# Operands of the MLP products of an encoder layer: from pairs of 32-bit planes to pairs of fp16 planes with scales found on the chip

## The chip, the cores and the metric

The kernel runs on one core of one Trainium2 chip. The metric is the device time of one execution in microseconds (us). A core has five engines that run side by side, each through its own instructions in order: TensorE (PE; its weight loads are shown apart as PEld), VectorE (DVE), ScalarE (ACT), GpSimd (POOL) and SyncE (SP). SP, ACT and POOL also issue DMAs, each on its own queue.

## What is computed

One layer of an encoder is applied to two sequences of 1024 and 512 tokens, 1024 features wide, in 32-bit floats. Two attention mixers come first; the change touches only the MLP behind them, and the norm that feeds it:

```python
def _rmsnorm(x, g):
    y = x * lax.rsqrt(jnp.mean(x * x, axis=-1, keepdims=True) + EPS)
    return y * g

h = h + _token_mixer(_rmsnorm(h, norm_mix_g), ...)          # attention, gates, projections
hn = _rmsnorm(h, norm_mlp_g)                                 # (1536, 1024)
h = h + jnp.square(jax.nn.relu(hn @ w_mlp_up)) @ w_mlp_down  # (1024, 4096), (4096, 1024)
out = _rmsnorm(h, norm_final_g)
```

## The kernel before, in words

Every 32-bit operand of a large product is held as two planes, `hi` and `lo`. `hi` is the value rounded to the 32-bit type that the code calls F32R (fp32r in the profile), `lo` is what is left. `mm3` (lines 273 to 276) makes a product of three matmuls: hi·hi, hi·lo, lo·hi. A plane pair is cut by two instructions: ACT copies the source into `hi`, and DVE subtracts `hi` from the source into `lo` (`cut`, lines 1564 to 1566).

The mixers of the two sequences run first, in a function `run` that is called once for each; at the end of the second, the norm for the MLP is formed token tile by token tile (gains in the tile `gb`), written to memory (`hnd`), read back as `hn` tiles, transposed by PE and cut into operands `B` (`pair_t`, lines 397 to 435).

`mlp` (from line 1541) computes the MLP with one level of a fast scheme that replaces 8 products of half-size blocks by 7. The 1536 tokens are two blocks `b` of 768 (384 columns in a half block). The up weights come in 16 chunks of 256 columns; one chunk of one block is a **stage**. `run_up` (line 1819) goes through the 16 stages of a block:

- `up_dma` (line 1587) loads the raw chunk `rawu` two chunks ahead on SP's queue, in two pieces of 512 KB.
- `up_steps` (line 1610) makes the seven operands A0 to A6 of the next chunk: four sums `S` on DVE and seven cuts. These steps are spread over the stage.
- `up` (line 1645) runs seven products of 4 x 3 matmuls with 384 columns: a (A0), b (A1), c (A2), d (A3), c again (A4), d again (A6), a again (A5). So a stage has 84 matmuls. Between them ACT and DVE empty PSUM: ACT copies `s` out of `ua` and `uc`, DVE adds, ACT takes relu and square (lines 1681 to 1685) and sends the result to memory (`ud`); DVE adds both halves (`cs`, line 1675), which SP stores.

Each engine takes its instructions in the order in which a scheduler put them when the kernel was built. In block 0, four stages (2, 4, 6 and 8) also hold a late norm of a token tile (`late_norm`, a sum of squares of 128x1024 on ACT, line 353).

Between the blocks stand three `pair_t` for block 1 and a first part of the down product (`dnf`, 144 matmuls of 512 columns). After block 1 the down product follows (`dn`, 1872 matmuls): stages of 6 x 12 matmuls with 512 columns, for which SP loads raw pieces `ar` (from `ud`) and `br` (down weights), DVE forms sums of them, and ACT and DVE cut them (`a_step`, line 1753, and `b_steps`, line 1773). DVE adds the results to the residual (`gain`), and a norm ends the kernel.

Of the kernel before, what the change touches and what calls it, by code (L numbers as in the profile page):

```python
# [11 lines left out]
F32 = mybir.dt.float32  # L12
# [62 lines left out]
def encoder(ctx: ExitStack, tc: tile.TileContext, xs, outs, w):  # L75
# [47 lines left out]
    gtab = cst.tile([P, 5, HD], F32, name="gtab")  # L123
    mhalf = cst.tile([P, 8], F32, name="mhalf")
# [3 lines left out]
    biases = dram.tile([8, 16, 8, 16, 48], F32, name="biases")  # L128

# [263 lines left out]
    def new_b(b, B):  # L393
        for i in range(7):
            B[i] = bbs[0].tile([P, 2, 4, HB], F32R, tag="bb", name=f"B{b}_{i}")

    def pair_t(nm, j, tiles, B, banks, tmp):
# [15 lines left out]
        def lo(i, src, eng=nc.vector):  # L413
            eng.tensor_tensor(B[i][:, 1, :, cols], v(src), B[i][:, 0, :, cols].bitcast(F32), op=ALU.subtract)
# [86 lines left out]
    def run(tr, nxt, first):  # L501
# [564 lines left out]
        with phase(f"phB{N}") as ph:  # L1066
# [228 lines left out]

            prep(0)
# [12 lines left out]
            for i in range(n + LS + LV):  # L1309
# [21 lines left out]
                fill.pull(f // 2)  # L1331
                if 0 <= i - LS < n:
                    t_unit(units[i - LS])
# [24 lines left out]
        with phase(f"phG{N}") as ph:  # L1358
# [72 lines left out]
            gb = gb[:, 0]  # L1431
            gn = None
# [6 lines left out]
            for half in range(2):  # L1439
                wo = wos[half]  # L1440
                hc = slice(half * 512, half * 512 + 512)
                for tt in range(NT):
# [65 lines left out]
                    if half == 1:  # L1508
# [5 lines left out]
                        if nxt is None:  # L1514
# [10 lines left out]
                            if 3 <= tt <= 5:  # L1525
                                j = tt - 3
                                if j == 2:
                                    a0 = first_a0.pop().tile([P, 2, 4, P], F32R, name="A0_0_0")
                                    nc.scalar.activation(a0[:, 0], a11, AF.Copy)
                                    nc.vector.tensor_tensor(a0[:, 1], a11, a0[:, 0].bitcast(F32), op=ALU.subtract)  # L1530
# [10 lines left out]
    def mlp():  # L1541
# [26 lines left out]

        def hn_load(b, j):
# [17 lines left out]
        def up_dma(st):  # L1587
            res = []
            for i in range(2):
                if st == (0, 0) and i == 1:  # L1590
# [10 lines left out]
                nc.sync.dma_start(  # L1601
                    r,
                    w["w_mlp_up"][0][i * 512 : (i + 1) * 512, st[1] * FB : (st[1] + 1) * FB].rearrange(
                        "(k p) c -> p k c", p=P
                    ),
                )
# [3 lines left out]
        def up_steps(st, ops):  # L1610
# [7 lines left out]
            def one(i):  # L1618
# [3 lines left out]
                t = k4.tile([P, 2, 4, P], F32R, tag="k4", name=f"A{nm}_{i}")  # L1622
# [11 lines left out]
                cut(t[:, 0], t[:, 1], src)  # L1634
# [10 lines left out]
        def up(st, A, B, side):  # L1645
# [27 lines left out]
            def total(half):  # L1673
                t = t2(f"cs{half}_{nm}")[:, 0:HB]
                nc.vector.tensor_tensor(t, kept[0, half], kept[1, half], op=ALU.add)
                nc.sync.dma_start(ud[b][2][fb // 4][fb % 4, :, half * HB : (half + 1) * HB], t)

            def put(f, half, src, in1=None):
# [6 lines left out]
                nc.scalar.activation(t, t, AF.Square)  # L1685
# [67 lines left out]
        def a_step(p, g, j):  # L1753
# [3 lines left out]
            hi, lo = (t2(f"a{n_}{p}_{g}_{j}", (P, 4, P), F32R) for n_ in "hl")  # L1757
            cut(hi, lo, r[0][:, :, (j % 2) * P : (j % 2 + 1) * P])
            a_hl[p, g, j] = (hi, lo)
# [13 lines left out]
        def b_steps(p, g):  # L1773
# [3 lines left out]
            def one(i):  # L1777
# [6 lines left out]
                t = k4.tile([P, 2, 512], F32R, tag="k4", name=f"wd{p}_{g}_{i}")  # L1784
                cut(t[:, 0], t[:, 1], src[:, i % 2, :])
# [33 lines left out]
        def run_up(b, A, B, last):  # L1819

            for fb in range(NFB):
                An = {}
                if fb + 2 < NFB:
                    up_dma((b, fb + 2))
                side = up_steps((b, fb + 1), An) if fb + 1 < NFB else []
                side = side + last(fb)
                if (b, fb) == (0, 0):
                    side = [[], []] + spread(side, 5)
                else:
                    side = spread(side, 7)  # L1830
                up((b, fb), A, B, side)
# [24 lines left out]
        def late_norm(r0):  # L1856
            xn = raw_k4(f"xnl{r0}")
            norm_to(xn, hl.pop(r0), gl[0][:, 0, :], f"l{r0}")
# [27 lines left out]
        for q in range(3):  # L1886
# [17 lines left out]
            for i in range(2):  # L1904
                j = 2 * q + i
                t = dp[:, i * 512 : i * 512 + 512]
                nc.scalar.activation(t, o[i], AF.Copy)
# [11 lines left out]

        hs = [bb.tile([P, 3, D], F32, tag="bb", name=f"hs{q}") for q in range(4)]  # L1920
# [46 lines left out]
        def final_last(o, e, t, before):  # L1967
# [15 lines left out]
            held(nc.vector.tensor_tensor(h[:, 0:512], o, h[:, 0:512], op=ALU.add))  # L1983
            square(ls, 1)
            before[0]()
            held(nc.vector.tensor_tensor(h[:, rs], e, h[:, rs], op=ALU.add))
# [29 lines left out]
        def gain(o, b, half, j):  # L2016
            t = b * NTB + j
            h = hs[t // 3][:, t % 3, half * 512 : half * 512 + 512]
            return nc.vector.tensor_tensor(h, o, h, op=ALU.add)
# [10 lines left out]
        for i, (p, g, j) in enumerate(order):  # L2030
# [16 lines left out]
            if i + 1 == len(order):  # L2047
# [10 lines left out]
                break  # L2058
            down_mm(acc[j], p, g, j, fresh, g == NG - 1)
# [7 lines left out]
            if g == NG - 1:  # L2067
                b, half = DEST[p][0]
                op = gain(acc[j], b, half, j)
# [4 lines left out]
                for b, half in DEST[p][1:]:  # L2074
                    todo.append(lambda o=acc[j], b=b, half=half, j=j: gain(o, b, half, j))
# [76 lines left out]
```

## Time and profile before

| | |
|---|---|
| median of 3 runs | 2090.28 us (2089.08 to 2093.42) |
| the profiled execution: its own time | 2090.06 us |
| its span (first to last instruction) | 2088.3 us |
| up product, block 0 / block 1 (about) | 1152 to 1386 us / 1423 to 1656 us |
| down product `dn` (about) | 1656 to 2080 us |

A profile is of one execution. A timeline row gives start, duration, engine, line, operation, output<-inputs, the shape and how many instructions were merged; in brackets stands how long the engine was idle before and what released it. A row of groups gives count, then busy time and mean duration, then idle time before. In a row for a tile or line the three numbers are the shortest, median and longest duration in ns. A row of windows gives for each stretch of time the busy time of PE, PEld, DVE, ACT and POOL, then the granted clock of TensorE (1.00 is full), the mean busy share of the 16 DMA engines and GB/s. Matmuls overlap: how often one starts says how fast PE goes, not how long one is shown.

### The profile page before, as it was taken

The page shows a single profiled execution, that of the slowest core. Times are in us where ns is not written, and L with a number is a line of the kernel's source. Part 1 is how long each engine was busy: PE and PEld are TensorE (multiplying, and loading weights), DVE is VectorE, ACT ScalarE, POOL GpSimd, SP SyncE. Part 2 cuts the span into 40 slices and gives each one's busy share as a digit, 9 for nine tenths or more (in the row PEclk, how much of TensorE's full clock was granted, in tenths as well). Part 3 has the DMA queues.
Part 4 walks back from the last instruction along what each step waited for, and adds up shares of the span by engine and source line. Part 5 has one row for each costly group of instructions (what it writes and reads, how often), then busy time and mean ns, then how long its engine had stood idle before and what let it go on. Part 6 is the DMA issues. An engine that isn't in the chain of part 4 may idle for free.

```text
span 2088.3 us, 31204 instructions
## 1 busy us (share of the span) xinstructions
PE 2062.2 (99%) x10521; PEld 1782.6 (85%) x10521; DVE 1495.9 (72%) x2885; ACT 1137.3 (54%) x2351; POOL 330.1 (16%) x445
## 2 busy tenths in 40 slices
PE   9999999999999999999999999999999999999998
PEld 8888878987797777877788999999999988888887
DVE  6775687778768856768855877787777777669563
ACT  5655654667647755666423665565655634334442
POOL 3232420422232212332002000011000000000000
PEclk9999999999999999999999999999999999999999
DMA  6546567645525555667754656477445899788561
GB/s 190 155 126 184 155 183 247 193 100 102 127 60 129 115 130 138 155 152 177 227 174 144 208 183 206 156 245 209 161 149 159 294 334 346 220 267 277 163 209 63
DMA packets 442569, 376.59 MB, mean 180 GB/s; under 512 B 167456, under 2 KB 380072, under 8 KB 442409
## 3 DMA queue, kind: packets, MB, share of 16 engines
q1 hardware_dynamic: 400471, 306.67, 50.6%
q10 hardware_dynamic: 36258, 50.88, 7.2%
q0 software_dynamic: 5680, 17.04, 2.9%
q8 instruction: 83, 1.36, 0.3%
q14 instruction: 77, 0.63, 0.1%
HBM read 263.29 MB, written 85.79 MB: 167 GB/s over the span
## 4 chain that ended last, share of the span: by engine, by line
PE 50%; DVE 1%; DMA 0%; issue 0%; ACT 0%; POOL 0%; POOLq 0%; ACTq 0%; DVEq 0%
PE dn L275 7%; PE dn L274 7%; PE dn L276 7%; PE uc L274 2%; PE ud L274 2%; PE ud L275 2%; PE uc L275 2%; PE ud L276 2%; PE uc L276 2%; PE ua L274 2%; PE ua L275 2%; PE ua L276 2%; PE ops L276 1%; PE ops L274 1%; PE ops L275 1%; PE ub L274 1%
## 5 line engine op out<-in xcount | busy, mean ns | idle before, releaser
L276 PE MATMUL dn<-wd,al 128*128 128x512 f32 (+1 forms) x624 | 242.3, 388 | 0.0
L275 PE MATMUL dn<-wd,ah 128*128 128x512 f32 (+1 forms) x624 | 242.3, 388 | 0.0
L274 PE MATMUL dn<-wd,ah 128*128 128x512 f32 (+1 forms) x624 | 242.3, 388 | 0.0
L1565 ACT ACTIVATE ah<-ar 128x512 fp32r<-128x512 f32 x168 | 104.3, 627 | 198.7 <-PE dn L275 179.4
L1566 DVE TENSOR_TENSOR al<-ar,ah 128x512 fp32r<-128x512 f32 x168 | 115.1, 693 | 73.9 <-ACT ah L1565 62.8
L274 PEld LDWEIGHTS dn<-wd,ah 128*128 128x128 f32 x624 | 117.1, 188 | 24.3
L276 PEld LDWEIGHTS dn<-wd,al 128*128 128x128 f32 x624 | 117.1, 188 | 24.2
L275 PEld LDWEIGHTS dn<-wd,ah 128*128 128x128 f32 x624 | 117.1, 188 | 24.1
L911 ACT ACTIVATE ps<-ss,nms 128x1024 f32<-128x1024 f32 (+1 forms) x96 | 93.2, 972 | 34.0 <-DVE ls L919 12.0
L908 DVE TENSOR_REDUCE nms<-ss 128x1 f32<-128x1024 f32 (+1 forms) x96 | 99.7, 1039 | 14.1 <-PE ss L906 13.4
L274 PE MATMUL gpss<-xs_0h,w_gs 128*128 128x512 f32 x256 | 102.5, 400 | 1.4 <-DVE ptls L946 1.3
L275 PE MATMUL gpss<-xs_0l,w_gs 128*128 128x512 f32 x256 | 100.8, 394 | 0.0
L276 PE MATMUL gpss<-xs_0h,w_gs 128*128 128x512 f32 x256 | 100.6, 393 | 0.0
L259 POOL TENSOR_TENSOR rs_f<-ms_f,mhalf 128x1 f32<-128x1 f32 x6 | 4.0, 668 | 590.7 <-DVE ms_f L255 590.7
L1565 ACT ACTIVATE A<-S 128x512 fp32r<-128x512 f32 x128 | 76.0, 623 | 29.6 <-DVE S L1628 25.4
L1164 POOL TENSOR_TENSOR bms<-rects,msks 128x384 f32<-128x384 f32 (+1 forms) x72 | 65.4, 919 | 152.0 <-DVE msbs L1180 98.4
L1684 ACT ACTIVATE c<-c 128x384 f32<-128x384 f32 x97 | 50.7, 524 | 68.3 <-DVE c L1683 68.3
L1566 DVE TENSOR_TENSOR A<-S,A 128x512 fp32r<-128x512 f32 x128 | 84.5, 686 | 3.5 <-ACT A L1565 3.5
L274 PE MATMUL uc<-B,A 128*128 128x384 f32 x256 | 85.6, 334 | 0.0
L274 PE MATMUL ud<-B,A 128*128 128x384 f32 x256 | 85.6, 334 | 0.0
L276 PE MATMUL ud<-B,A 128*128 128x384 f32 x256 | 85.5, 334 | 0.0
L275 PE MATMUL ud<-B,A 128*128 128x384 f32 x256 | 85.5, 334 | 0.0
(391 smaller groups left out, 6311.9 us busy)
## 6 DMA issues: line engine op xcount, KB each, us to landing
ar<-ud SPq DMA_DIRECT2D x120, 512.0 KB
br<-in_w_mlp_down_dram SPq DMA_DIRECT2D x72, 512.0 KB
rawu<-in_w_mlp_up_dram SPq DMA_DIRECT2D x64, 512.0 KB
ud<-c ACTq DMA_DIRECT2D x128, 192.0 KB
raw_gs<-in_w_in_dram SPq DMA_DIRECT2D x32, 512.0 KB
zgs<-sgs ACTq DMA_DIRECT2D x48, 256.0 KB
ud<-cs SPq DMA_DIRECT2D x64, 192.0 KB
vss<-vds SPq DMA_DIRECT2D x256, 32.0 KB
```

The source lines that it names most:

```text
L259: nc.gpsimd.tensor_tensor(r[:, :n], m[:, :n], mhalf[:, :n], op=ALU.pow)
L274: nc.tensor.matmul(out, ah, bh, start=start, stop=False, **kw)
L275: nc.tensor.matmul(out, ah, bl, start=False, stop=False, **kw)
L276: nc.tensor.matmul(out, al, bh, start=False, stop=stop, **kw)
L908: nc.vector.tensor_reduce(nm_, s, axis=AX.X, op=ALU.max, negate=True)
L911: nc.scalar.activation(p, s, AF.Exp, bias=nm_, accum_out=l)
L1164: nc.gpsimd.tensor_tensor(bm.rearrange("p (r c) -> p r c", c=32), rects[h][:, ir : ir + kr_n, jr : jr + 32], msk[:, hf * 3 + ct, :].rearra ...
L1565: nc.scalar.activation(hi, src, AF.Copy)
L1566: nc.vector.tensor_tensor(lo, src, hi.bitcast(F32), op=ALU.subtract)
L1684: nc.scalar.activation(t, t, AF.Relu)
```

## The change

All operands of the up and down products become pairs of fp16 planes: `hi` is the value times a scale, rounded to fp16, `lo` the rest of the scaled value in fp16. The scales must keep every value within the range of fp16, so they are found from bounds:

- The gain row `gb` is scaled by its own maximum; the squared activations are unscaled by the chunk's inverse (in the square, line 1820) and each result of the down product by the inverse of its two scales (in `gain`, by a multiply-add).
- For each up chunk of block 0 (block 1 uses the same scales) ACT sums the absolute values of the rows of the raw chunk, in two instructions (`row_sums`, line 1630: `abs_0`, `abs_1`). POOL adds the two sums, SP writes the 128 sums to memory (`wmd`) and reads them back to every partition (`top`), DVE takes the maximum, and POOL forms the scale and its inverse (three small instructions). Only then can A0 of this chunk be cut. This is asked for at the end of the stage two chunks ahead and taken in the stage after it. For chunks 0 and 1 it is done during the second sequence's mixer (`first_scales`).
- The down weights are read once more, in 32 pieces of 512 KB, for their row sums (`down_sums`, `abswd`): seven loads and then one more into halves of the B tiles that fp16 leaves empty, one sum in each of the stages 3 to 10 of block 0, and two in each of the stages 0 to 11 of block 1.
- The maxima of the activations come from the instruction that forms `cs`, which now also takes a row maximum. Five more round trips through memory (`find_scale`) turn them and the weights' sums into scales.

```diff
+    def ask_top(row, src, n, pool_tile):
+        nc.sync.dma_start(wmd[row : row + 1, 0 : n * P].rearrange("o (n p) -> p (o n)", p=P), src)
+        back = pool_tile[:, 0 : n * P]
+        nc.sync.dma_start(back, wmd[row : row + 1, 0 : n * P].to_broadcast([P, n * P]))
+        return back
+    def set_scale(back, k, dst, inv, tmp):
+        nc.vector.tensor_reduce(tmp, back, axis=AX.X, op=ALU.max)
+        nc.gpsimd.tensor_scalar(inv, tmp, 1e-30, k / VTOP, op0=ALU.add, op1=ALU.mult)
+        nc.gpsimd.tensor_tensor(dst, inv, svs[:, 14:15], op=ALU.pow)
...
+        def cut16(hi, lo, src, by):
+            nc.scalar.activation(hi, src, AF.Copy, scale=by)
+            nc.vector.scalar_tensor_tensor(lo, src, by, hi, op0=ALU.mult, op1=ALU.subtract)
+        def row_sums(raw, n, nm):
+            junk = t2(f"abs{nm}", (P, 1024), BF16)
+            nc.scalar.activation(junk, raw, AF.Abs, accum_out=col(n))
+        def chunk_scale(fb):
...
+            def ask():
+                n = 32 + 2 * (fb % 8)
+                nc.gpsimd.tensor_tensor(col(n), col(n), col(n + 1), op=ALU.add)
+                got.append(ask_top(fb, col(n), 1, t2(f"top{fb}")))
+            def take():
+                set_scale(got.pop(), 4.0, col(fb), col(16 + fb), col(n))
+                nc.gpsimd.tensor_scalar(col(16 + fb), col(16 + fb), svs[:, 17:18], 1.0, op0=ALU.mult, op1=ALU.mult)
...
-                t = k4.tile([P, 2, 4, P], F32R, tag="k4", name=f"A{nm}_{i}")
+                t = k4.tile([P, 2, 2, 4, P], F16, tag="k4", name=f"A{nm}_{i}")[:, 0]
...
-                cut(t[:, 0], t[:, 1], src)
+                cut16(t[:, 0], t[:, 1], src, col(st[1]))
...
-                nc.vector.tensor_tensor(t, kept[0, half], kept[1, half], op=ALU.add)
+                nc.vector.tensor_tensor_reduce(
+                    out=t, in0=kept[0, half], in1=kept[1, half], op0=ALU.add, op1=ALU.max, scale=1.0, scalar=0.0,
+                    accum_out=col(64 + 32 * b + 2 * fb + half),
+                )
...
-                nc.scalar.activation(t, t, AF.Square)
+                nc.scalar.activation(t, t, AF.Square, scale=col(16 + fb))
...
+                elif take is not None:
+                    side = [[take]] + spread(side, 6)
                 else:
                     side = spread(side, 7)
+                take = None
+                for n, steps in scales_of(b, fb).items():
+                    side[n] += steps
+                if new is not None:
+                    for n, step in zip((4, 5, 5), (*new[0], new[1])):
+                        side[n].append(step)
+                    take = new[2]
```

In the built program each matmul with fp16 operands is two instructions of PE, a weight load and the matmul, where there was one. What ACT does within a stage is in another order. These are ACT's instructions before, in stage 5 of block 0, from the second copy `s` on (`A_6` and `A_7` are cuts for chunks 6 and 7, `c` the relu and square):

```order
L1700 ACTIVATE s_0_5_13647<-uc_5_13644 128x384
L1565 ACTIVATE A_6_3_13719<-S_0_6_13683 128x512
L1684 ACTIVATE c_0_5_13723<-c_0_5_13723 128x384
L1685 ACTIVATE c_0_5_13723<-c_0_5_13723 128x384
L1565 ACTIVATE A_6_4_13740<-S_0_6_13684 128x512
L1686 DMA ud_1_1_12795<-c_0_5_13723 128x384
L1565 ACTIVATE A_6_6_13764<-rawu_6_1_13476 128x512
L1684 ACTIVATE c_0_5_13744<-c_0_5_13744 128x384
L1565 ACTIVATE A_6_5_13784<-rawu_6_1_13476 128x512
L1685 ACTIVATE c_0_5_13744<-c_0_5_13744 128x384
L1565 ACTIVATE A_7_0_13817<-rawu_7_0_13636 128x512
L1686 DMA ud_0_1_12791<-c_0_5_13744 128x384
```

In that place A0 of chunk 7 is cut before stage 5 ends, as soon as the raw chunk lies there. The same engine now, in stage 7, from its second row sum on (`abs_1` is the second sum of raw chunk 9, `abswd` a sum of down weights):

```order
L1625 ACTIVATE A_8_5_14242<-rawu_8_1_13904,gtab 128x512
L1821 DMA ud_0_1_12824<-c_0_7_14196 128x384
L1630 ACTIVATE abs_1_14219,gtab<-rawu_9_1_14081 128x1024
L1816 ACTIVATE c_0_7_14245<-ua_7_14086 128x384
L1820 ACTIVATE c_0_7_14245<-c_0_7_14245,gtab 128x384
L1819 ACTIVATE c_0_7_14225<-c_0_7_14225 128x384
L1821 DMA ud_0_1_12824<-c_0_7_14245 128x384
L1820 ACTIVATE c_0_7_14225<-c_0_7_14225,gtab 128x384
L1821 DMA ud_1_1_12828<-c_0_7_14225 128x384
L1827 ACTIVATE s_0_8_14258<-ua_8_14254 128x384
L1625 ACTIVATE A_9_0_14293<-rawu_9_0_14079,gtab 128x512
L1625 ACTIVATE A_9_1_14296<-S_0_9_14298,gtab 128x512
```

The sum `abs_1` of chunk 9 stands behind all seven cuts of chunk 8, and the first cut of chunk 9 stands eight instructions behind that sum, with the first copy `s` of stage 8 between. SP's instructions now, around the end of stage 5 (`wmd` is the write of the 128 sums, `top` the read back; what a row waits for stands in brackets):

```order
L1811 DMA ud_2_1_12832<-cs_0_5_13866 128x384 [waits DVE_49]
L150 DMA rawu_8_1_13904<-in_w_mlp_up_dram 128x4x256 [waits DMAHW0_49,DVE_49]
L138 DMA wmd<-gtab 128x1 [waits DMAHW1_49,Pool_49]
L140 DMA top_13875<-wmd 128x128 [waits DMAHW3_49,DMAHW2_49,DMAHW1_49]
L1811 DMA ud_2_1_12832<-cs_0_5_13926 128x384 [waits DMAHW5_49,DVE_49]
```

The write and the read back stand directly behind the second 512 KB piece of a raw chunk on the same queue. And DVE's instructions now, where stage 5 ends (line 145 is the maximum over `top`):

```order
L1818 TENSOR_TENSOR c_0_5_13878<-ud_5_13742,u_0_5_13745 128x384 [waits PE_49]
L145 TENSOR_REDUCE gtab<-top_13875 128x1 [waits DMAHW2_49,DMAHW1_49,Pool_49]
L1807 ISA cs_0_5_13926,gtab<-c_0_5_13898,c_0_5_13878 128x384 [waits Activation_49]
L1807 ISA gtab 128x1
L1759 TENSOR_TENSOR S_0_7_13950<-rawu_7_0_13732,rawu_7_1_13734 128x512 [waits DMAHW3_49]
L1760 TENSOR_TENSOR S_0_7_13951<-S_0_7_13950,rawu_7_0_13732 128x512 [waits DVE_49]
```

The maximum waits for the read back, and the sums `S` of the next chunk stand behind it.

More of the change, by code (lines that the diff above doesn't have):

```diff
@@ L128, in encoder, with col, up_raw, first_scales @@
     biases = dram.tile([8, 16, 8, 16, 48], F32, name="biases")
+    wmd = dram.tile([32, 256], F32, name="wmd")
+    def col(n):
+        return sc[:, n : n + 1]
+    def ask_top(row, src, n, pool_tile):
[7 more added lines that the diff above has]
+        nc.gpsimd.tensor_tensor(dst, inv, svs[:, 14:15], op=ALU.pow)
+    def up_raw(raw, fb, i):
+        nc.sync.dma_start(
+            raw,
+            w["w_mlp_up"][0][i * 512 : (i + 1) * 512, fb * FB : (fb + 1) * FB].rearrange("(k p) c -> p k c", p=P),
+        )
+    def first_scales():
+        nc.gpsimd.memset(svs[:, 14:15], -1.0)
+        for fb in range(2):
+            for i in range(2):
+                raw = rawp.tile([P, 1024], F32, tag="raw", name=f"rawt{fb}_{i}")
+                up_raw(raw.rearrange("p (k c) -> p k c", c=FB), fb, i)
+                yield
+                nc.vector.tensor_reduce(
+                    col(32 + 2 * fb + i), raw, axis=AX.X, op=ALU.max, apply_absolute_value=True
+                )
+        for fb in range(2):
+            back = ask_top(fb, sc[:, 32 + 2 * fb : 34 + 2 * fb], 2, rawp.tile([P, 1024], F32, tag="raw", name=f"top{fb}"))
+            yield
+            set_scale(back, 4.0, col(fb), col(16 + fb), col(32 + 2 * fb))
+            nc.gpsimd.tensor_scalar(col(16 + fb), col(16 + fb), svs[:, 17:18], 1.0, op0=ALU.mult, op1=ALU.mult)
     def row_bcast(dst, src, n, rep=1):
@@ L1294, in v_unit @@
                 late.append(cut)
+            fsc = first_scales() if not first else iter(())
             prep(0)
@@ L1331, in run @@
                 fill.pull(f // 2)
+                if i >= 5 and i % 2:
+                    next(fsc, None)
                 if 0 <= i - LS < n:
@@ L1431, in run @@
             gb = gb[:, 0]
+            if first:
+                nc.vector.tensor_reduce(svs[:, 16:17], gb, axis=AX.X, op=ALU.max, apply_absolute_value=True)
+                nc.vector.tensor_scalar(
+                    svs[:, 17:18], svs[:, 16:17], 1e-30, 4.0 * D**0.5 / VTOP, op0=ALU.add, op1=ALU.mult
+                )
+                nc.vector.reciprocal(svs[:, 16:17], svs[:, 17:18])
+            nc.scalar.activation(gb, gb, AF.Copy, scale=svs[:, 16:17])
             gn = None
@@ L1566, in cut @@
             nc.vector.tensor_tensor(lo, src, hi.bitcast(F32), op=ALU.subtract)
+        def cut16(hi, lo, src, by):
[5 more added lines that the diff above has]
+        def chunk_scale(fb):
+            raw = raw_up[0, fb]
+            got = []
+            def ask():
[3 more added lines that the diff above has]
+            def take():
+                n = 32 + 2 * (fb % 8)
+                set_scale(got.pop(), 4.0, col(fb), col(16 + fb), col(n))
+                nc.gpsimd.tensor_scalar(col(16 + fb), col(16 + fb), svs[:, 17:18], 1.0, op0=ALU.mult, op1=ALU.mult)
+            sums = [
+                lambda i=i: row_sums(
+                    raw[i].rearrange("p k c -> p (k c)"), 32 + 2 * (fb % 8) + i, f"{fb}_{i}"
+                )
+                for i in range(2)
+            ]
+            return sums, ask, take
@@ new lines, in mlp, with down_sums, find_scale, ask @@
+        spare = {}
+        def down_sums(n):
+            g, i, r_ = n // 4 % NG, n % 4, n // 16
+            raw = spare[n % 7].rearrange("p a k c -> p (a k c)")[:, 0 : 2 * D].bitcast(F32)
+            nc.sync.dma_start(raw, wd_v[r_, g, :, i, :])
+            return lambda: row_sums(raw, 128 + n, f"wd{n}")
+        def find_scale(row, src, k, dst, inv, tmp):
+            got = []
+            def ask():
+                nc.vector.tensor_reduce(col(tmp), src, axis=AX.X, op=ALU.max)
+                got.append(ask_top(row, col(tmp), 1, t2(f"top{row}")))
+            return ask, lambda: set_scale(got.pop(), k, col(dst), col(inv), col(tmp))
@@ L2014, in final_scale, with gain @@
             return [partial(left, c0) for c0 in range(0, 512, width)] + [right]
-        def gain(o, b, half, j):
+        def gain(o, b, half, j, p):
             t = b * NTB + j
             h = hs[t // 3][:, t % 3, half * 512 : half * 512 + 512]
-            return nc.vector.tensor_tensor(h, o, h, op=ALU.add)
+            by = col(INV[5 if p == 5 else "r"])
+            return nc.vector.scalar_tensor_tensor(h, o, by, h, op0=ALU.mult, op1=ALU.add)
         DEST = {5: [(0, 1)], 3: [(1, 1)], 1: [(1, 0)], 6: [(1, 1), (0, 0), (0, 1)], 7: [(0, 1)], 4: [(0, 0)], 2: [(1, 0)]}
@@ L2068, in mlp @@
                 b, half = DEST[p][0]
-                op = gain(acc[j], b, half, j)
+                op = gain(acc[j], b, half, j, p)
                 if p == 2:
```

84 lines of the change are left out of this document (64 added, 20 removed).

## The prediction, made before the changed kernel had run

> **What bounds the kernel now.** The page's first part comes first, and beside it the one row in which PE waits anywhere from 1100 us to the end:
>
> ```profile
> PE 2062.2 (99%) x10521; PEld 1782.6 (85%) x10521; DVE 1495.9 (72%) x2885; ACT 1137.3 (54%) x2351; POOL 330.1 (16%) x445
> ...
> PE pt L402 <- ACT B L411: 0.4, 2, 0.2
> ```
>
> PE is the bound, and in the part that the change touches it waits 0.4 us in all. So every nanosecond that a matmul gets shorter counts in full, and so does every wait that the change gives PE. How fast PE goes is read from starts in its timeline. The pairs below are 12 up matmuls apart, 27 down matmuls apart, and, as the mixer has fp16 products already, 4 fp16 matmuls apart:
>
> ```profile
> 1250.48 0.33 PE L274 MATMUL ud<-B,A 128*128 128x384 f32 x1
> 1252.56 0.33 PE L274 MATMUL ua<-B,A 128*128 128x384 f32 x1
> ...
> 1699.79 0.39 PE L275 MATMUL dn<-wd,ah 128*128 128x512 f32 x1
> 1705.91 0.39 PE L275 MATMUL dn<-wd,ah 128*128 128x512 f32 x1
> ...
> 467.75 0.38 PE L963 MATMUL os<-PTs,vpls 128*128 128x512 f16 x1
> 468.61 0.38 PE L963 MATMUL os<-PTs,vpls 128*128 128x512 f16 x1
> ```
>
> The pitch is 173.3 ns at 384 columns, 226.7 ns at 512, and 215.0 ns at 512 in fp16. The first two differ by 0.417 ns a column, which leaves 13.3 ns that do not depend on columns; fp16 leaves 1.7 ns.
>
> A stage of the up product lasts 84 x 0.1733 = 14.56 us, as two copies of `ua` show, one stage apart. The windows (times as in the table's explanation) show what else is busy in block 0, in block 1 and in the first `dn` stages:
>
> ```profile
> 1227.80 0.49 ACT L1692 ACTIVATE s<-ua 128x384 f32<-128x384 f32 x1 [0.77 <-PE ua L276]
> 1242.36 0.49 ACT L1692 ACTIVATE s<-ua 128x384 f32<-128x384 f32 x1 [0.76 <-PE ua L276]
> ...
> 1200.00:1300.00 100.00, 100.00 (x579) 100.00 (x578) 75.30 (x131) 62.18 (x124) 4.48 (x8) 1.00 0.61 196
> 1500.00:1600.00 100.00, 100.00 (x578) 100.00 (x578) 71.56 (x124) 59.28 (x118) 0.00 (x0) 1.00 0.47 150
> 1656.00:1680.00 24.00, 24.00 (x108) 19.98 (x108) 16.13 (x25) 13.57 (x25) 0.00 (x0) 1.00 1.02 344
> 1680.00:1700.00 20.00, 20.00 (x90) 16.55 (x89) 16.06 (x24) 6.50 (x11) 0.00 (x0) 1.00 1.08 355
> 1760.00:1780.00 20.00, 20.00 (x90) 16.57 (x89) 16.62 (x25) 11.38 (x20) 0.00 (x0) 1.00 0.91 313
> ```
>
> In block 0 DVE is at 75%, ACT at 62% and the DMA engines at 0.61, in block 1 at 72%, 59% and 0.47: all have time over. From 1656 to 1780 us the DMA engines have none (1.02, 1.08, 0.91).
>
> **The matmuls.** The up product has 2 x 16 x 84 = 2688, the down product 1872 + 144 = 2016, together 4704. Each loses 13.3 - 1.7 = 11.6 to 11.7 ns, so PE saves 4704 x 0.0117 = 55.0 us, if nothing makes it wait. A stage is then 84 x 0.1616 = 13.6 us. The Trainium skill ("TensorE: Matmul & The Clock Gate", Back-to-back issue gap) gives N/2.4 + 2.5 ns between starts, that is 215.8 and 162.5 ns; by it the saving would be 51 us. The row's 215.0 agrees within a nanosecond, and the sum keeps 55.0.
>
> **The scale loop of block 0** is the dearest addition. By ACT's order now, the two sums of chunk n+1 come behind all seven cuts of chunk n, and the first cut of chunk n+1 needs the round trip that starts behind these sums. So each stage has one loop that nothing can shorten: seven cuts, two sums, POOL, write, read, DVE, POOL, and the next cuts. If a loop is longer than a stage of PE, PE waits for the difference. Its ACT part comes from these rows (a sum of squares over 1024 stands in for the new sums of 1024):
>
> ```profile
> 1219.87 1.05 ACT L353 ACTIVATE xnl<-hl 128x1024 f32<-128x1024 f32 x1
> ...
> 1220.91 0.51 ACT L1684 ACTIVATE c<-c 128x384 f32<-128x384 f32 x1
> 1221.32 0.62 ACT L1565 ACTIVATE A<-rawu 128x512 fp32r<-128x512 f32 x1
> 1221.84 0.51 ACT L1685 ACTIVATE c<-c 128x384 f32<-128x384 f32 x1
> 1222.26 0.51 ACT L1684 ACTIVATE c<-c 128x384 f32<-128x384 f32 x1
> ...
> L1565 ACT ACTIVATE A<-S x128: 613/624/636, 1155.3 to 1637.7; 128x512 fp32r<-128x512 f32 x128
> L923 ACT ACTIVATE hls<-ps,rcs x64: 708/712/737, 448.5 to 735.5; 128x512 f16<-128x512 f32 x64
> ```
>
> From start to start a sum takes 1.04 us, a relu 0.41, a cut 0.52, a square 0.42. The mixer's copy to fp16 with a scale from a column takes 712 ns where the cut takes 624, so a cut will take 0.61 and a square 0.52. Seven cuts 4.3, one `s` 0.4, two pairs of relu and square 1.9, two sums 2.1: 8.7 us. The other activations of a stage fall into the return path. Laying out the order by hand, I add 1.0 us in which ACT waits for DVE, because the sums `S` stand behind the maximum on DVE and are the next cuts' sources; that is my estimate, between 0 and 2.
>
> The return path has no row of its own. POOL's small operations, and the smallest DMA with its first user, are:
>
> ```profile
> L259 POOL TENSOR_TENSOR rs_hs<-ms_hs,mhalf x8: 560/562/572, 356.3 to 1127.4; 128x1 f32<-128x1 f32 x8
> ...
> L143 ACTq DMA_DIRECT2D grow<-in_norm_mix_g_dram x1: 537/537/537, 0.7 to 0.7; - x1
> L156 PEld LDWEIGHTS grow<-grow,ones x4: 284/330/332, 2.8 to 4.7; 1*128 1x128 f32 x4
> ...
> L908 DVE TENSOR_REDUCE nms<-ss 128x1 f32<-128x1024 f32 x64 | 77.8, 1216 | 7.7 <-PE ss L906 7.2
> ```
>
> The 4 KB of `grow`, asked for at 0.7 us, are used at 2.8: at most 2.1 us. I take 2.1 for the write and for the read, since both are small too. The reduce of 1024 takes 1.22; for 128 I estimate 0.25. Return path: POOL 0.56, two DMAs 4.2, DVE 0.25, two POOL operations 1.1, and 0.3 for hand-overs (an estimate): 6.4 us. The bounds for one DMA are wide: 0.54 us (issue alone) and, for 512 KB in a busy stretch, the 5 us between the following two rows (issue, and first user):
>
> ```profile
> 999.14 0.33 SPq L1020 DMA_DIRECT2D rawos<-obds  x1
> 1004.19 1.06 ACT L263 ACTIVATE oXs<-rawos 128x1024 fp32r<-128x1024 f32 x1 [1.31 <-DMA rawos<-obds]
> ```
>
> So a loop takes 8.7 + 1.0 + 6.4 = 16.1 us. In eight stages a sum over down weights (1.04) stands among the cuts, and in four a late norm does (1.04): 12 x 1.04 over 13 loops, on average +1.0. The mean loop is 17.1 us against 13.6: PE waits 3.5 us in each of 13 loops, **45.5 us**. From this go 5 us: chunks 0 and 1 have their scales from the mixer, and the first loop starts early in stage 0, so that its end is about 5 us ahead (by hand; 0 to 9). Behind the last loop the cuts for `dnf` on the same ACT come late: +3 (0 to 8). Net **+43.5**. What hid the cuts before was the whole stage ahead of their use; that cover is what the loop takes away.
>
> **What stays hidden.** Block 1 has no loop. Its ACT work per stage is 59% of 14.56 = 8.6 us before and gains 7 x 0.09 for cuts, 4 x 0.1 for squares and at most 2.1 for sums: about 11.7 of 13.6. DVE's cut becomes the operation of the second row:
>
> ```profile
> L1566 DVE TENSOR_TENSOR A<-S,A x128: 679/684/695, 1156.3 to 1638.6; 128x512 fp32r<-128x512 f32 x128
> L924 DVE SCALAR_TENSOR_TENSOR hls<-ps,rcs,hls x64: 727/747/1211, 450.2 to 736.3; 128x512 f16<-128x512 f32 x64
> L1180 DVE DVE_READ_ACCUMULATOR2_ANT msbs<- x96: 73/82/85, 182.5 to 1003.4; 128x1 f32 x96
> ```
>
> At 747 for 684 ns seven cuts cost 0.4 us, and the two row maxima with `cs` 0.2 (a read of the accumulator each): DVE goes in block 0 from 75% of 14.56, 10.9, to 11.8 with the maximum, of 13.6, and in block 1 it has less to do. If that cover were gone, the 0.85 us would count in each stage. The extra 16.8 MB of down weights (32 x 512 KB) fall into stages whose DMA share is 0.61 and 0.47. The multiply-add in `gain` costs 0.06 a piece beside PE: nothing.
>
> **The down product's start.** Until 1780 us DMA sets the pace as much as PE, and DVE waits for its raw pieces:
>
> ```profile
> DVE ar L1756 <- DMA ar<-ud: 28.8, 19, 3.4
> ```
>
> PE would save 5.2% of these 124 us, 6.4. A transfer that already runs at 1.0 can't come sooner, but its buffers come free sooner and the wait is not yet PE's. I give back most: **+5** (0 to 8).
>
> **The entry.** The seven loads of down weights stand ahead of or beside the first raw chunks, and PE's first chunk is already close behind the raw load:
>
> ```profile
> 1150.90 0.63 ACT L1565 ACTIVATE A<-rawu 128x512 fp32r<-128x512 f32 x1 [1.80 <-DMA rawu<-in_w_mlp_up_dram]
> 1154.62 0.33 PE L274 MATMUL ue<-B,A 128*128 128x384 f32 x1
> ```
>
> ACT waits 1.80 us for it, and PE needs a cut of it 3.7 us later. With four reduces of 1.22 us on DVE in the mixer: **+2** (0 to 6).
>
> **The sum**, against the profiled execution's own 2090.06 us, which lies 0.2 below the median of the runs: 2090.06 - 55.0 + 43.5 + 5 + 2 = 2085.6; I forecast 2085. A measurement can tell about 0.2%, 4.2 us, from no change; so "same" is 2086.1 to 2094.5, and the forecast lies just below that band: the sign hangs on the loop alone. At 17.45 us a loop the change is worth nothing.
>
> **Rivals.** *The loop is short.* DVE's sums come in time (no 1.0) and a small DMA takes 1.5 us: 14.9 us a loop, 1.3 x 13 = 17 of waits less the 5 of lead, and nothing late at the end: 2090.06 - 55 + 12 + 5 + 2 = 2054. For it speaks that no row shows a small DMA longer than 2.1 us, and that this one holds the issue too. Against it, the queue is not empty here as it was there. Chance 0.22.
>
> *The small write waits behind the raw piece*, the slower side. On SP's queue it stands directly behind 512 KB. At 344 GB/s (first `dn` window) these take 1.5 us; if the write must wait for them, each loop is 18.6 and the time 2085.6 + 13 x 1.5 = 2105. The Trainium skill ("DMA: Bandwidth & Descriptors", Queues, rings and completion order) says that on each DMA engine descriptors are taken in ring order, which is this mechanism. The trace has no small DMA behind a large one on one queue; that the raw piece may have landed long before POOL is done with the sums speaks against it. It decides from 0.35 us a loop on. Chance 0.28.
>
> *The change does not do what it says:* pairs of fp16 keep the pitch of 173.3 and 226.7 ns. Then a stage stays 14.56, loops cost 2.5 x 13 = 33, less 5, plus 3, and 2090.06 + 31 + 2 = 2123. The mixer's 215.0 speaks against it. Chance 0.03.
>
> **Chances and range.** The forecast has 0.45, in a range of its own of 2072 to 2098 (1 us more or less per loop); 0.02 is left for what I don't see. The range reaches into both rivals, 2057 to 2111. Faster than 2086.1: the short loop and half of the forecast's case, 0.43; between 2086.1 and 2094.5, 0.16; slower, 0.41.
>
> **What would show it.** Right: stages of block 0 of about 17 us with a PE gap of some 3.5 us before the first matmul of each, released by ACT's cut of A0 or A1; stages of 13.6 in block 1; `dn` matmuls 215 ns apart; two DMAs `wmd` and `top` of about 2 us each. Wrong: block 0 stages of 13.6 to 15 (short loop), a `wmd` landing that follows the raw piece's (queue), PE waits in block 1 (ACT or DVE out of time), or a pitch above 220 ns.

## The result, and the profile after

The changed kernel takes 2278.71 us (median of 4 runs, 2274.87 to 2284.39), the kernel before 2090.35 us: a ratio of 1.0901 (95% interval 1.0874 to 1.0928). The forecast was 2085 with a range up to 2111; the slowest rival stood at 2123. So the sign was wrong, and the time lies beyond every case that I had priced. The profiled execution has a span of 2273.1 us against 2088.3, 184.8 us more. Its page begins:

```profile
PE 2058.7 (91%) x10521; PEld 1409.3 (62%) x10521; DVE 1532.7 (67%) x2982; ACT 1245.9 (55%) x2474; POOL 363.7 (16%) x521
...
PE   9999999999999998999996555557899989999998
PEclk9999999999999999999997787778999999999999
```

PE was 99% busy and is now 91%, and the lost part lies in one place: seven of 40 slices, which are block 0 of the up product, and there the granted clock falls too. PE's waits over the whole span (total, times, longest), and below them ACT's from 1150 to 1560 us:

```profile
PE ua L315 <- ACT A L1625: 79.8, 9, 10.1
PE uc L315 <- ACT s L1835: 75.4, 8, 16.1
```

```profile
ACT A L1625 <- POOL gtab L147: 162.1, 13, 14.9
ACT A L1625 <- DVE S L1762: 13.7, 13, 2.1
```

PE waits for cuts, or for a copy `s` that stands behind the cuts on ACT, and ACT waits 13 times, 12.5 us each, for the scale that POOL makes (line 147). So the scale loop is the bound of block 0, as the prediction had it; but it is much longer. One whole loop, from the timeline of ACT, POOL, SP and DVE:

```profile
1256.66 0.72 ACT L1625 ACTIVATE A<-rawu,gtab 128x512 f16<-128x512 f32 x1 [10.29 <-POOL gtab L147]
...
1267.53 0.19 ACT L1630 ACTIVATION_READ_ACCUMULATOR abs<-rawu 128x1 f32 x1
...
1267.80 0.19 POOL L1638 TENSOR_TENSOR gtab<-gtab 128x1 f32<-128x1 f32 x1 [10.74 <-ACT abs L1630]
...
1267.51 0.38 SPq L150 DMA_DIRECT2D rawu<-in_w_mlp_up_dram  x1
1268.02 0.43 SPq L138 DMA_DIRECT2D wmd<-gtab  x1
1276.73 0.33 SPq L140 DMA_DIRECT2D top<-wmd  x1
...
1280.06 0.29 DVE L145 TENSOR_REDUCE gtab<-top 128x1 f32<-128x128 f32 x1 [12.11 <-DMA top<-wmd]
...
1280.94 0.89 POOL L147 TENSOR_TENSOR gtab<-gtab,svs 128x1 f32<-128x1 f32 x1
...
1281.87 0.72 ACT L1625 ACTIVATE A<-rawu,gtab 128x512 f16<-128x512 f32 x1 [11.18 <-POOL gtab L147]
```

Seven cuts, sums and what lies between take ACT from 1256.66 to 1267.72: 11.1 us. The way back takes 14.2: from the issue of the write `wmd` to that of the read `top`, which waits for it, 8.7 us; from there to DVE's maximum 3.3; then 1.8 to the next cut. Over the 13 loops (starts of the maximum from 1200.70 to 1562.19) the mean is 27.8 us (the loop shown is the shortest); over the 14 trips the write's mean is 10.0 (8.3 to 12.1) and the median of the read 3.7.

Where the 184.8 us lie, by the first or last matmuls of each part in the two traces: the mixers end 12.8 us later, PE's first product of raw weights comes another 4.3 later, block 0 takes 414.8 us instead of 232.8 (+182.0), from the first `dnf` to the first `dn` 262.3 instead of 269.3 (-7.0), and `dn` 415.3 instead of 423.0 (-7.7). In block 0 PE's waits make 159 us; the other 256 hold 1344 matmuls that take 219 at full speed (the granted clock has a mean of 0.79 there).

### The profile page after: what moved, and what is told of

Same layout as the page of the kernel before. It is cut to its first block, busy times and chain, and to the rows that moved or that the text cites. A ratio compares the mean times of both kernels' runs of the same rounds, so it can differ in the third digit from the quotient of the medians.

```text
span 2273.1 us, 31474 instructions
## 1 busy us (share of the span) xinstructions
PE 2058.7 (91%) x10521; PEld 1409.3 (62%) x10521; DVE 1532.7 (67%) x2982; ACT 1245.9 (55%) x2474; POOL 363.7 (16%) x521
## 5 line engine op out<-in xcount | busy, mean ns | idle before, releaser
L317 PE MATMUL dn<-wd,a 128*128 128x512 f16 (+1 forms) x624 | 237.9, 381 | 4.6 <-DVE a L1626 4.6
L315 PE MATMUL dn<-wd,a 128*128 128x512 f16 (+1 forms) x624 | 237.9, 381 | 2.8 <-ACT a L1625 1.5
L316 PE MATMUL dn<-wd,a 128*128 128x512 f16 (+1 forms) x624 | 237.8, 381 | 0.0
L315 PEld LDWEIGHTS <-A 128*128 128x128 f16 x896 | 90.9, 102 | 151.3 <-ACT A L1625 87.9
L316 PEld LDWEIGHTS <-A 128*128 128x128 f16 x896 | 90.8, 101 | 148.6 <-issue 96.2
L1625 ACT ACTIVATE a<-ar,gtab 128x512 f16<-128x512 f32 x168 | 113.3, 712 | 116.3 <-DVE ar L1891 41.3
L315 PE MATMUL ua<-B,A 128*128 128x384 f16 x252 | 87.7, 349 | 84.8 <-ACT A L1625 79.8
L315 PE MATMUL uc<-B,A 128*128 128x384 f16 x256 | 89.9, 351 | 75.4 <-ACT s L1835 75.4
L317 PEld LDWEIGHTS <-A 128*128 128x128 f16 x896 | 90.8, 101 | 72.0 <-issue 10.2
L1626 DVE SCALAR_TENSOR_TENSOR a<-ar,gtab,a 128x512 f16<-128x512 f32 x168 | 121.4, 756 | 18.3 <-ACT a L1625 18.3
L317 PEld LDWEIGHTS <-a 128*128 128x128 f16 x676 | 66.5, 98 | 87.1 <-DVE a L1626 7.6
L315 PEld LDWEIGHTS <-a 128*128 128x128 f16 x676 | 66.5, 98 | 81.3 <-ACT a L1625 2.3
L316 PEld LDWEIGHTS <-a 128*128 128x128 f16 x676 | 66.6, 98 | 80.9 <-issue 3.4
L1625 ACT ACTIVATE A<-S,gtab 128x512 f16<-128x512 f32 x128 | 87.7, 712 | 47.4 <-DVE S L1762 36.9
L315 PE MATMUL gpss<-xs_0h,w_gs 128*128 128x512 f32 x256 | 102.5, 400 | 1.3 <-DVE ptls L989 1.3
L1626 DVE SCALAR_TENSOR_TENSOR A<-S,gtab,A 128x512 f16<-128x512 f32 x128 | 92.5, 746 | 13.1 <-ACT A L1625 13.0
```

The costliest lines, as they stand in the source:

```text
L315: nc.tensor.matmul(out, ah, bh, start=start, stop=False, **kw)
L316: nc.tensor.matmul(out, ah, bl, start=False, stop=False, **kw)
L317: nc.tensor.matmul(out, al, bh, start=False, stop=stop, **kw)
L1625: nc.scalar.activation(hi, src, AF.Copy, scale=by)
L1626: nc.vector.scalar_tensor_tensor(lo, src, by, hi, op0=ALU.mult, op1=ALU.subtract)
```

## The experiments

My theory after the result: the round trip in series is the loss, and in it the write. Its rivals: ACT and DVE have too much work in block 0; or the write is slow only because of its queue.

**No round trip** (e1), and then **no write** (e2). In e1 the chunks 2 to 15 take the scales of chunks 0 and 1; nothing bounds their values then. In e2 the read still waits for the sums, through POOL, but reads a row that was written in the mixer.

```diff
-                cut16(t[:, 0], t[:, 1], src, col(st[1]))
+                cut16(t[:, 0], t[:, 1], src, col(st[1] % 2))
...
-                    for n, step in zip((4, 5, 5), (*new[0], new[1])):
+                    for n, step in zip((4, 5), new[0]):
```

> The chunks 2 to 15 use the scales of chunks 0 and 1, so the sums stay but the round trip through memory (POOL, write, read, maximum, POOL) is left out in block 0. Theory (the round trip in series is the loss): the 13 loops of 27.8 us become stages of 13.6, 13 x 14.2 = 185 us go, 2075 to 2100 us; PE has no gaps in block 0 and its clock is full there. Rival (ACT or DVE has too much work in block 0, or PE's lower clock comes from the fp16 matmuls themselves): above 2150 us, with PE still waiting for cuts.

> Each loop of block 0 reads back a row that was written during the mixer; the write is left out, so the scale is that of chunk 0 or 1, but the read still waits for the chunk's own sums. Theory (the write of 128 single numbers is the dear part, about 9 of the 14 us): loops of about 19 us, 13 x 9 = 117 us less, 2150 to 2175 us. Rival (the read, or any small transfer while raw pieces are under way, is as dear): loops of 23 us or more, above 2210 us.

2092.43 us and 2142.44 us. Without the trip 186 of the 188 us go: the theory holds, the rival does not. The windows of the changed kernel and of e1, from 1200 to 1400 us, show PE's gaps closed and its clock back (0.77 and 0.99); ACT is at 82% there:

```profile
1200.00:1400.00 200.00, 120.20 (x614) 64.59 (x615) 88.14 (x166) 94.77 (x173) 19.37 (x40) 0.77 0.37 102
```

```profile
1200.00:1400.00 200.00, 190.97 (x1153) 112.35 (x1152) 153.23 (x285) 164.89 (x309) 8.00 (x16) 0.99 0.59 186
```

With the read alone the loop is 18.7 us (13 loops from 1194.07 to 1436.85), 9.1 less: the write is the dear half. The time lies 8 us below its band. Of the 136 us saved the 13 loops make 118, and 9 are the first of the 14 trips, which stands ahead of these loops (the first maximum starts 20.1 us after the first product of block 0, not 29.0). That PE's clock stays higher (a mean of 0.982 against 0.957) may be the reason for the rest, and was not tried by itself.

**Another queue** (e3: the write on ACT's queue; e4: both on POOL's):

```diff
-        nc.sync.dma_start(wmd[row : row + 1, 0 : n * P].rearrange("o (n p) -> p (o n)", p=P), src)
+        eng = nc.scalar if 2 <= row < 16 else nc.sync
+        eng.dma_start(wmd[row : row + 1, 0 : n * P].rearrange("o (n p) -> p (o n)", p=P), src)
```

> The write of the sums goes out on ACT's queue instead of SP's, the read stays on SP's. Theory A (the write is slow because it stands behind a 512 KB piece on SP's queue): it lands in 2 to 3 us, loops of about 21 us, about 2190 us. Theory B (it is slow by its own form, 128 pieces of 4 bytes to memory): still about 9 us, 2265 to 2295 us.

> Write and read back both go out on POOL's queue. Theory A (SP's queue): write and read land in 2 to 3 us each, loops of about 20 us, 2170 to 2200 us. Theory B (the form of the write): the write still takes about 9 us, and POOL's issues add about 1 us a loop, 2265 to 2310 us.

2268.38 and 2271.71 us; the write's median is 9.2 and 9.5 us. My rival of the queue is refuted: the write is as slow with no raw piece ahead of it. (The order in which one queue's pieces are taken is not disproved by this; it is only not what costs here.)

**Fewer, joined, or spread pieces** (e9, e10, e11). e9 writes 64 of the 128 sums. e10 lets PE turn the column of sums into a row, which then is one piece of 512 bytes. e11 writes the 128 sums 512 bytes apart, reads one row back, and takes the scale of chunk 0 or 1 after that:

```diff
+                nc.tensor.transpose(tr[0:1, :], col(n), ident)                # e10
+                nc.vector.tensor_copy(row, tr[0:1, :])
+                nc.sync.dma_start(wmd[fb : fb + 1, 0:P], row)
...
+        apart = dram.tile([P, P], F32, name="apart")                          # e11
+                nc.sync.dma_start(apart[:, 0:1], col(n))
+                nc.sync.dma_start(back, apart[0:1, :].to_broadcast([P, P]))
```

> The changed kernel, but in block 0 only 64 of the 128 sums are written and read back. Theory A (the write's time is its count of pieces, one after the other, some 65 ns each): it lands in 4 to 5 us instead of 8.5, 13 x 4 = 52 us less, 2215 to 2235 us. Theory B (a fixed time of such a write): still 8 us or more, 2262 to 2282 us.

> The changed kernel, but in block 0 PE turns the 128 sums into one row first (as in e7), DVE copies it to memory on the chip, and SP writes the row in one piece of 512 bytes and reads it back as before. Theory A (the write of one number from each of 128 partitions is what is slow): it lands in 2 to 3 us, a loop of 20 to 22 us, 2165 to 2210 us. Theory B (every write to memory that someone waits for takes 7 us or more while the other transfers run): loops of 27 us or more, 2260 to 2300 us.

> The changed kernel, but in block 0 the 128 sums are written 512 bytes apart, and the read back takes the first of these rows; the scale is that of chunk 0 or 1, formed after the read back. Theory A (the 128 pieces of the old write collide in the same 512 bytes of memory): the write lands in 2 to 4 us, loops of 20 to 22 us, 2165 to 2210 us. Theory B (one number from each of 128 partitions is slow wherever it goes): still about 9 us, loops of 26 us or more, 2250 to 2290 us.

| | write (median of 14, us) | read (median of 14, us) | loop (mean of 13, us) | time (us) |
|---|---|---|---|---|
| changed kernel | 9.9 | 3.7 | 27.8 | 2278.7 |
| e9: 64 numbers | 8.7 | 3.1 | 26.0 | 2248.93 |
| e10: one piece of 512 bytes | 1.4 | 3.4 | 21.2 | 2182.40 |
| e11: 128 numbers, 512 bytes apart | 3.7 | 3.0 | 22.0 | 2194.18 |

SP's rows of e10 (`row`) and of e11 (`apart`), each write with the read that waits for it:

```profile
1229.99 0.24 SPq L1647 DMA_DIRECT2D wmd<-row  x1
1231.07 0.32 SPq L1649 DMA_DIRECT2D top<-wmd  x1
```

```profile
1247.96 0.42 SPq L1642 DMA_DIRECT2D apart<-gtab  x1
1251.43 0.33 SPq L1644 DMA_DIRECT2D top<-apart  x1
```

One piece lands in 1.1 us here and in 1.4 at the median. The same 128 numbers from 128 partitions take 9.9 us into one run of 512 bytes and 3.7 into places 512 bytes apart. So most of the write's time comes from where the pieces go, not from their number. The records of DMA packets in the two traces show where it is spent: the 4-byte packets start between 2.1 and 3.0 us after the issue of the write in the loop shown of the changed kernel, and between 2.2 and 2.9 in that of e11, but the read follows the last of them by 5.7 us in the one and by 0.6 in the other. The pieces leave as fast; what differs is the time until their landing is told. e9 fell between its theories: half the pieces save 1.2 us on the write and 0.6 on the read, and the loops make 13 x 1.8 = 23 of its 30 us. The Trainium skill ("DMA: Bandwidth & Descriptors", Specifications) says that transfers under 512 bytes are done by reading, modifying and writing back. That agrees with 9.9 against 3.7, if pieces that modify the same run hold each other up. But if they simply followed one another, half of them should take about half the time, and e9's 8.7 is not that; how they collide stays open.

**No memory at all** (e7): PE turns the column into a row in the free columns of a PSUM bank, DVE takes the maximum, a second small matmul spreads it.

```diff
+                tr = free_bank[0][:, HB : HB + P]
+                nc.tensor.transpose(tr[0:1, :], col(n), ident)
+                nc.vector.tensor_reduce(sc[0:1, n : n + 1], tr[0:1, :], axis=AX.X, op=ALU.max)
...
+                nc.tensor.matmul(tr[:, 0:1], onesr[0:1, :], sc[0:1, n : n + 1], start=True, stop=True, skip_group_check=True)
```

> The changed kernel, but in block 0 the round trip does not go through memory: PE turns the column of sums into a row in a free part of a PSUM bank, DVE takes its maximum, PE spreads it to 128 partitions, DVE and POOL make the scale. Theory: the return path falls from 14 to 4 or 5 us, loops of 15 to 16 us, 2100 to 2140 us. Rival (PE takes its instructions in order and stands at the two small matmuls until the sums are there): waits of PE at these, above 2170 us.

2108.09 us, loops of 15.5 us (14 scales from 1193.17 to 1394.25). The way back, in POOL's, PE's and ACT's rows:

```profile
1301.55 0.19 POOL L1642 TENSOR_TENSOR gtab<-gtab 128x1 f32<-128x1 f32 x1 [10.78 <-ACT abs L1630]
...
1302.27 0.27 PE L1644 MATMUL ub<-ident,gtab 128*1 128x128 f32 x1
1302.96 0.38 PE L1651 MATMUL ub<-gtab 1*128 1x1 f32 x2
...
1304.43 0.71 ACT L1625 ACTIVATE A<-rawu,gtab 128x512 f16<-128x512 f32 x1
```

2.9 us instead of 14.2. This full search of scales is still 17 us slower than the kernel before on that chip (2090.66). Its block 0 takes 242.2 us, 9.5 more than before: 13 loops of 15.5 against stages of 13.6 cost 25, and the shorter matmuls give 14. Its mixers end 17.1 us later than before and the first product of raw weights comes another 4.6 later, which is more than the 13 us that the parts behind block 0 save.

**What else is paid** (e5, e6, f1, f2). e5 is e1 without the 28 row sums; e6 leaves out the first scales in the mixer too; f1 keeps of those only loads and reduces, f2 only the trips (with constants, so their writes wait for nothing):

```diff
-                if new is not None:
-                    for n, step in zip((4, 5, 5), (*new[0], new[1])):
...
-            back = ask_top(fb, sc[:, 32 + 2 * fb : 34 + 2 * fb], 2, rawp.tile([P, 1024], F32, tag="raw", name=f"top{fb}"))
+            nc.gpsimd.memset(col(fb), 1.0 / 1.2e-5)
+            nc.gpsimd.memset(col(16 + fb), 1.2e-5)
```

> As e1 (chunks 2 to 15 use the scales of chunks 0 and 1, no round trip), and the 28 row sums of 1.04 us that ACT makes of raw up chunks in block 0 are left out too. Theory (in e1 ACT at 83% and DVE wait for each other, and PE for both): block 0 loses the most part of its 12 us of waits and their cold starts, 2070 to 2082 us. Rival (the waits of e1 in block 0 have another cause): 2087 to 2094 us.

> As e5, and the scales of chunks 0 and 1 are constants too, so that nothing of the scale search is left in the second sequence's mixer: no loads, no four reduces, no two round trips on SP's queue. Theory (the mixer is 12 to 14 us late because SP waits some 9 us for a write before each read back, with the mixer's loads behind it): the last mixer product starts at about 1152 us again instead of 1166, and 10 to 15 us less than e5. Rival (the new pools or the order of the mixer cost it): within 4 us of e5.

> As e5, with constants as the scales of chunks 0 and 1: the four loads and reduces in the mixer stay, the two round trips are left out. Theory (the loads and reduces, which take buffers and DVE time of the mixer, are its 8 us): the mixer's products between 853 and 894 us of before are 8 us late as in e5, within 3 us of e5's 2084. Rival (the trips): no lag there, 2074 to 2079 us.

> As e5, with the four loads and reduces left out and constants sent on the two round trips, which stay on SP's queue. Theory (the loads and reduces cost it): no lag between 853 and 894 us, 2072 to 2078 us. Rival (the trips): the lag of 8 us stays, within 3 us of e5's 2084.

e5: 2083.97, short of its band by 2 us. Block 0 takes 224.2 us where e1 needs 238.3, so the sums' work on ACT is worth 14 us there, 8 in the total (on two chips). e6: 2072.83, 11.1 less than e5, but not as expected: the mixer's last product starts at 1161.7, not 1152, and in e5 at 1163.8. So only 2 of the 11.1 us lie in the mixers; the rest lies behind them, most of it from the first `dnf` to the end of `dn`, which the edit does not touch.

A mixer product that stands at 852.9 us before and one at 893.9 are 8.5 us further apart in the changed kernel, 7.5 to 9.2 in e1, e2, e5 and e7, and as before in e6. f1: 2078.26, with 2.1 us of this lag; f2: 2073.50, with 0.7. That looks as if neither half made the lag alone, but f2 did not leave its writes in place: with constants they went out at 627 and 629 us. SP's and PE's rows of the changed kernel show what stands there:

```profile
851.39 0.43 SPq L138 DMA_DIRECT2D wmd<-gtab  x1
...
854.81 6.71 SPq L1252 DMA_TRANSPOSE bhs<-hbs  x1
...
864.84 0.58 PE L1294 MATMUL obs<-bhs,vss 128*128 128x512 f16 x1 [6.69 <-ACT pbs L1227]
```

It is the second small write of the first scales. A transposing load `bhs` behind it takes 6.7 us to issue where the median is 1.2, until 10.1 us after the write went out, and PE then waits 6.7 us. In all 13 runs that have this write there, PE has such a wait, 5.8 to 7.5 us long, which ends 12.1 to 13.6 us after the write; f1, f2 and e6 have none over 2.0. So the lag goes with the same slow write. A run that moves this write alone was not made.

**Towards a better version** (b2, b3, b4). b2 is e5 with the first trips on POOL's queue; in b3 the down loads of block 0 wait for the stage before them; in b4 POOL, not ACT, scales the gain row of the late norms.

```diff
+                nc.gpsimd.tensor_scalar(raw[:, 0:1], after, 0.0, 0.0, op0=ALU.mult, op1=ALU.add)      # b3
...
-                nc.scalar.activation(gl[0][:, 0, :], gl[0][:, 0, :], AF.Copy, scale=svs[:, 16:17])
+                nc.gpsimd.tensor_scalar(gl[0][:, 0, :], gl[0][:, 0, :], svs[:, 16:17], 1.0, op0=ALU.mult, op1=ALU.mult)
```

> As e5 (scales of chunks 0 and 1 for all chunks, no up sums in block 0), and the two round trips of the first scales go out on POOL's queue. Theory (in the mixer SP stands 8.9 us at the read back, with the loads of the next heads behind it): the 8 us between 853 and 894 us go, 2072 to 2079 us. Rival (the trip itself or POOL's work is in the way): 2081 to 2088 us.

> As b2, but the seven loads of down weights that stood ahead of or beside the first raw chunks are made to wait for a result of stages 1 to 8 of block 0. Theory (they delay the first raw pieces, so that PE waits 4.2 to 4.6 us for the first chunk's cut and starts at a lower clock): PE waits under 1 us there, 5 to 8 us less than b2. Rival (the first chunk is late for another reason): within 2 us of b2.

> As b3, but the one instruction of ACT that scales the gain row for the late norms (it stands ahead of the first chunk's cuts and waits 7.7 us for the row's load) is done by POOL. Theory (this instruction, not the raw loads, makes the first cuts late): PE waits under 1 us for the first chunk, and no cold start follows, 4 to 7 us less than b3, 2070 to 2074 us, a ratio to the kernel before of about 0.991. Rival (the raw load itself is late): PE still waits over 3 us there, within 2 us of b3.

b2: 2082.39 (ratio 0.9956, 0.9941 to 0.9971): the lag stays at 9.1 us, with a wait of 7.1 that ends 13.2 us after the write, now on POOL's queue. So SP's wait at the read back is not its cause. (The profiled execution took 2092.04, the five others 2082.06 to 2082.46; the trace shows the slowest.) b3: 2077.81 (0.9939, 0.9918 to 0.9959), 4.6 us less than b2, but PE still waits 4.1 us for the first chunk's cut, so not by the mechanism that I named, and by which is open. b4 finds what makes this cut late. ACT's rows of the changed kernel, and then of b4, behind the last operand `B`:

```profile
1160.14 1.14 ACT L454 ACTIVATE B<-ta 128x512 f16<-128x512 f32 x2
1169.86 1.15 ACT L2009 ACTIVATE gbl<-gbl,svs 128x1024 f32<-128x1024 f32 x1 [8.57 <-DMA gbl<-in_norm_mlp_g_dram]
1170.91 0.71 ACT L1625 ACTIVATE A<-rawu,gtab 128x512 f16<-128x512 f32 x1
```

```profile
1166.66 1.14 ACT L454 ACTIVATE B<-ta 128x512 f16<-128x512 f32 x2
1169.77 0.72 ACT L1625 ACTIVATE A<-rawu,gtab 128x512 f16<-128x512 f32 x1 [1.97 <-DMA rawu<-in_w_mlp_up_dram]
```

In the changed kernel the first cut starts 10.8 us after the last `B`, in b4 3.1 us, and PE's wait of 4.1 us is gone. The time is not less for it: 2077.77 us (0.9938, 0.9922 to 0.9954), where 2070 to 2074 was expected; six runs scatter from 2073.0 to 2084.1. b3 and b4 are 0.6% faster than the kernel before, at a price: they use scales from chunks 0 and 1 for all chunks, and the range of the others is taken on trust. The version that searches every scale (e7) beats neither e1 nor the kernel before.

## Why the prediction was wrong, step by step

**The matmuls: right, a little large.** In the changed kernel 11 up matmuls and 18 down matmuls lie between these rows:

```profile
1270.98 0.33 PE L315 MATMUL ua<-B,A 128*128 128x384 f16 x1
1272.77 0.33 PE L317 MATMUL ua<-B,A 128*128 128x384 f16 x1
...
1999.88 0.38 PE L315 MATMUL dn<-wd,a 128*128 128x512 f16 x1
2003.77 0.38 PE L315 MATMUL dn<-wd,a 128*128 128x512 f16 x1
```

162.7 and 216.1 ns, 10.6 less than before, 50 us in all instead of 55. Four matmuls were too few to read 215.0 from. The Trainium skill ("TensorE: Matmul & The Clock Gate", Back-to-back issue gap) has a formula, N/2.4 + 2.5 ns for the gap of one matmul, that gives 162.5 and 215.8, which was nearer.

**The scale loop: the mechanism right, the write mis-sized.** The failed step is "I take 2.1 for the write and for the read, since both are small too". The read took 3.7 and the write 10.0. The row behind the 2.1 was a read of one run of 4 KB; the write puts 128 separate numbers into one run of 512 bytes, and no row of the trace showed such a thing. The upper bound, 5 us, came from a large transfer, and size was taken as the worst that could happen to a DMA. That is 9.5 of the 10.7 us by which the loop missed 17.1; ACT's part, 11.1 in the loop shown with its sum over down weights, had been put at 10.7. In 13 loops the miss is 139 us. The same write stands twice in the mixer, where the entry counted loads and reduces only. The break-even of 17.45 us a loop does not hold either: at 15.5 us the sum gives 2085.6 - 13 x 1.6 = 2064.8, and e7 took 2108.09. With the other terms as measured (-50, 11 for the ends, 9, 12 and 17, all below) only a loop as short as a stage breaks even, and e1, without loops, is about there.

**The lead and the end of block 0.** Block 0 lost 196 us beside its matmuls (182.0 and 14). The 13 loops of 27.8 against stages of 13.6 make 185, the ends 11, where I had -5 and +3. Some 8 of the 11 lie at the start and are the write of the first of the 14 trips: the first maximum starts 29.0 us after the first product of block 0, in e10, with its short write, 21.1. From the last maximum to the first `dnf` the two have 24.3 and 24.5.

**What hid: in part.** From the first `dnf` to the first `dn` 7.0 us are saved where the matmuls give 16, and I had costed nothing: PE waits 3.3 us there for `hn` loads and a first cut, and in block 1 another 4.9 for ACT and DVE. In e1 block 0, without a loop, still loses 20 us: 11.5 are waits of PE, most of the rest falls into stretches of half clock. With ACT at 82% and DVE close behind they hand over to each other too closely; e5, with less work for ACT, loses 6. Cover like block 1's ("about 11.7 of 13.6") was not enough there.

**The down product's start: +5 said, +12 measured** (423.0 to 415.3, where the matmuls give 20): 7.3 us of waits for cuts and `hs`, and 10 us of half clock near its start.

**The entry: +2 said, +17 measured**: 12.8 in the mixers and 4.3 at the first chunk. Of the 12.8 the lag at the second small write makes 8.5, and 4.0 stand already at 852.9 us. The saving to be had is less sure: builds differ by as much. At 445 us, in the first sequence's mixer, they are 0.3 to 4.8 us late, and e6, without the lag, is 8.0 late at 852.9 and 9.5 at the end of the mixers. The 4.3 are an instruction that I had not costed: the scaled gain row, one ACT instruction, stood in ACT's order ahead of the first cuts and waited for its load. All five together, -50 + 196 + 9 + 12 + 17, make 184 of the 184.8 us.

**The rivals.** The queue had 0.28 and was wrong. It put the loss in the right instruction for a wrong reason, so that its price was 1.5 us a loop, where the write took 7.9 more than the 2.1. The short loop (0.22) missed to the other side, and the old pitch (0.03) is ruled out by 162.7. None of them had a loop near 27.8: that belongs to the 0.02 that I had left over.

## What to carry to other kernels

A price from a row of the same size is not enough for a DMA: compare the form, how many separate pieces, how long each, and whether they fall into the same run of memory. A round trip that stands in series with each stage deserves the widest bounds of the whole sum, and a way around it (here PE and PSUM, 2.9 us instead of 14.2) is worth knowing before the stage is built around it. Go through the new order of each engine at the start of a part, too: one instruction that waits for a load holds all that stands behind it. And a small gap between builds is not yet an effect: look for it in the part that the edit touches.

## What the runs showed of the hardware

128 numbers of 4 bytes from 128 partitions took 9.9 us into one run of 512 bytes of memory, 8.7 for 64 of them, 3.7 when they went 512 bytes apart, and 1.4 as one piece from one partition (medians). SP's, ACT's and POOL's queues made no difference over 0.7 us. In the mixer a transposing load issued on SP's queue behind such a write took 5.7 to 6.7 us to issue in ten runs, where the median is 1.2.

After a wait PE starts slowly. In the changed kernel, behind a wait of 9.55 us, the trace has 25 matmuls at about 0.32 us, twice the pitch, before the rest went at 0.163:

```profile
1282.64 0.50 PE L315 MATMUL ua<-B,A 128*128 128x384 f16 x1 [9.55 <-ACT A L1625]
...
1291.38 0.52 PE L315 MATMUL ub<-B,A 128*128 128x384 f16 x1
1291.70 0.37 PE L315 MATMUL ud<-B,A 128*128 128x384 f16 x1
1291.90 0.33 PE L316 MATMUL ud<-B,A 128*128 128x384 f16 x1
```

From 1282.64 to 1291.70 that is 9.1 us, where 25 matmuls at 0.163 take 4.1. The granted clock stood at a half from 1278.1 to 1291.8. The Trainium skill ("TensorE: Matmul & The Clock Gate", Part 1: The HAM clock gate) has PE at half clock after about 3.4 us of idling and at full clock after about as long of work. The trace agrees on the half, but here the slow part lasted 9.1 us, with a further short wait of 0.78 us in it. All 15 stretches of half clock in block 0 last 3.41 us or a multiple of it, up to 17.1. No step of the prediction had counted this; how much of block 0's loss it makes beside the loop was not separated.

Not settled: by what way the small write holds a transposing load, how its pieces collide in one run of memory, and how much of e9's and e2's gain beyond the loop is PE's clock. Which stages need the down sums where they are was not tried.
